# A hybrid encoder layer on one core: the next down weights' transfers go through ScalarE's queue a period later, the last two pairs' activation lows through VectorE, and the next group's sums behind them

## The chip, the cores and the metric

One core of one Trainium2 chip runs the whole layer. The metric is device time in microseconds (us) of one execution. The time before is the median of three runs, 820.84 us (819.92 to 821.39). The profile is of one further execution of the same program.

## What is computed

The reference is one encoder layer on 512 positions of width 1024, in float32:

```
x = x + 0.5 * (silu(h1 @ w_gate1) * (h1 @ w_up1)) @ w_down1      # h1 = RMSNorm(x), d_ff = 2752
h = RMSNorm(x); u = h @ w_in                                     # Fourier group, q, k, v
x = x + concat([fourier_mixer(u), gqa_attention(u)]) @ w_out
x = x + 0.5 * (silu(h2 @ w_gate2) * (h2 @ w_up2)) @ w_down2      # h2 = RMSNorm(x)
y = RMSNorm(x)
```

The change touches only the two feed-forward parts (FFN 1 and FFN 2).

## The kernel before

**High and low parts.** Every matrix product is made of float32r operands split in two: a high part (a rounded copy) and a low part (the value less its high part). A weight tile comes from HBM as a raw float32 tile. ScalarE casts it to the high part (line 182 for down weights, 404 for gate and up weights). The low part is made in one of two ways. `lows` (line 140) has VectorE subtract the high part from the raw value. `rest_by_dma` (lines 169 and 170) has ScalarE write the negated high part, and GpSimd issues a DMA that adds the raw value onto it on the way.

**Pairs and groups.** The 2752 hidden columns are 21 pairs of 128 gate and 128 up columns, and a tail. They are taken in four groups for each FFN (lines 38 and 39). The first group is multiplied plainly. In the other three, `seven` (line 440) multiplies each pair by a seven-product scheme on half-blocks: the products are P0 to P5 and P9, written to banks r, p, q and c (lines 449 and 452), and four sums of weight blocks (`c1` to `c4` of `prepare`, line 419) are their operands. P0 of a pair needs the block a11, of which the low part comes by the accumulating DMA (tile `ring<-raw_g`). One pair takes TensorE one period of somewhat over 9 us. The `TABLE` (line 46) lists the steps of one period; a `+` behind a name means the step of the next pair, a `-` the one of the pair before. ScalarE, VectorE and GpSimd keep this order; TensorE and SyncE keep the order in which the code is written; outside the table a scheduler places the instructions.

**Down products.** When a group's pairs are through, their activations (tile `at`, high and low part, from u by lines 518 and 521 or 522) are multiplied by the down weights of the group, eight blocks d = 0 to 7 (`dn` on line 196, 18 products for a block of six pairs), and added to x (line 629). The raw down weights, `raw_dn_d`, share three buffers (tag "raw", line 163) with the raw up weights, `raw_u`, in the order in which the code asks for them. The raw gate weights, `raw_g`, have two buffers of their own.

**Around the end of a group.** In `seven`, `i` counts the pairs of the group and `len(js)` is their number. At P0 of the last pair (line 531) `load_below` asks SyncE for raw_dn 0 and 1. At the table's `c3+` in the last period and at its `t.h` in the extra half period behind it (`BELOW`, lines 43 and 533), `below` makes the casts and lows of down blocks 0 and 1. The low part of an activation is the table's step `nh`: it comes by accumulating DMA (tile `at<-u`, line 522), except for the last pair of a group, and the last two of an FFN's last group, which take VectorE (line 543). The next group's first pair is prepared during the down products, its steps (`FIRST`, line 45) tied by `behind` (line 619) to come after the instructions in `anchors`: ScalarE's copy pA and VectorE's sum lB of the last pair.

Of the kernel before, what the change touches and what calls it, by code (L numbers as in the profile page):

```python
# [18 lines left out]
KD = D // P  # L19
# [20 lines left out]
PLACES = 7  # L40
HALF = S // 2
USES = "a11", "a12", "s2", "s1", "s4", "s3", "a22"
BELOW = "t.h", "c3"
HELD = 2
FIRST = ("ld", "a.h", "a.l", "c1", "d.h", "d.l", "c2", "c3", "c4", "s.h", "s.l", "t.h", "t.l")
TABLE = """
# [47 lines left out]
def asf(ap):  # L94
    return ap.bitcast(F32)
# [3 lines left out]
def encoder(ctx, tc, A, out):  # L99
    nc = tc.nc  # L100
# [38 lines left out]
    def lows(lo, src, hi):  # L139
        return nc.vector.tensor_tensor(out=lo, in0=src, in1=asf(hi), op=ALU.subtract)  # L140
# [17 lines left out]
    def weight_slots(n=KD, skip=0):  # L158
        c = slice(skip, skip + n * P)
        return (slot()[:, c].rearrange("p (a b) -> p a b", b=P) for _ in range(2))  # L160

    def raw_tile(src, name, n=KD):
        raw = wp.tile([P, KD, P], F32, tag="raw", name=f"raw_{name}")
        nc.sync.dma_start(out=raw[:, :n, :], in_=src)
        return raw

    def rest_by_dma(lo, hi, src):

        nc.scalar.activation(lo, asf(hi), AF.Copy, scale=-1.0)  # L169
        nc.gpsimd.dma_start(out=lo, in_=src, accum_op=ALU.add)  # L170
# [5 lines left out]
    def weights(src, name, n=KD, raw=None, by_dma=False, skip=0):  # L176
        raw = raw or raw_tile(src, name, n)
        hi, lo = weight_slots(n, skip)
        if name in HI_DVE:
            nc.vector.tensor_copy(hi[:, :n, :], raw[:, :n, :])  # L180
        else:
            nc.scalar.copy(hi[:, :n, :], raw[:, :n, :])  # L182
        if by_dma:
            rest_by_dma(lo, hi, src)
        else:
            lows(lo[:, :n, :], raw[:, :n, :], hi[:, :n, :])
        return hi, lo

    def turned(ap):
# [104 lines left out]
    def ffn(norm, after, wgu, wd, wdt, groups, opening, closing):  # L294
# [4 lines left out]
        n_ = norm.n  # L299
        n_plain = len(groups[0])  # L300
        with tc.tile_pool(name=f"act{n_}", bufs=1) as ap, tc.tile_pool(name=f"sums{n_}", bufs=2) as sp:
# [8 lines left out]
            def place(j):  # L310
                where[j] = free.pop(0)
                return where[j]
# [8 lines left out]
            def gate(c, between={}, by_dma=False):  # L321
                with ExitStack() as behind:
                    for i in (norm.squared, norm.added) if n_ and c else ():
                        behind.enter_context(tc.issue_after(i.ins))
                    whi, wlo = weights(wgu[c], f"gu{n_}_{c}", by_dma=by_dma)
                ps = bank(f"gu{n_}_{c}")
                for k in range(KD):
                    between.get(k, int)()
                    product(ps, whi[:, k, :], wlo[:, k, :], hh[k], hl[k], k == 0, k == KD - 1, turn=True)
                return ps  # L330
# [38 lines left out]
            def back(ts):  # L369
                plain[:] = [t for t in plain if all(t is not q for q in ts)]  # L370
# [67 lines left out]
            anchors = {}  # L438

            def seven(js, first, finish, load_below, below):  # L440
# [86 lines left out]
                def do(i, name):  # L527
                    shift = name.count("+") - name.count("-")
                    name = name.rstrip("+-")
                    i += shift  # L530
                    if i == len(js) - 1 and name == "P0":
                        load_below()
                    if i == len(js) and name in BELOW:
                        below()
                    if i not in range(len(js)):
                        return
                    o = state.setdefault(i, {})
                    if "w" not in o:
                        o.update(prepare(js[i]))
                    if "P0" not in o:  # L540
                        o.update(evacuation(js[i], o))
                    if i and (i, name) != (1, "ld") or not i and name not in FIRST:
                        o["l" if name == "nh" and i >= len(js) - 1 - last else name]()
                    if i == 0 and name == "P0":
                        finish()

# [6 lines left out]
                def rest():  # L553
                    for name in ended:
                        do(len(js), name)

                return rest

            def down_raw(d, group, gi):

                js = [j for j in group if j != "t"]
                return raw_tile(wd[d][:, js[0] : js[-1] + 1, :], f"dn{n_}_{d}_{gi}", len(js))

            def down(d, group, gi):

                js = [j for j in group if j != "t"]
                src, halves_ = wd[d][:, js[0] : js[-1] + 1, :], closing and gi == len(groups) - 1 and d >= KD - LAST
                raw = raws[d] = loads.pop(0) if loads else down_raw(d, group, gi)
                whi, wlo = weights(src, "", len(js), raw, skip=SKIP if halves_ else 0)
                if halves_:  # L570
                    token_weights(d, js)
                w = wt[d // 4][:, d % 4 * P : (d % 4 + 1) * P]

                def steps(ps, t):
                    for i, j in enumerate(group):
                        h, l = (at[:, where[j], o, t] for o in range(2))
                        first, last = i == 0, i == len(group) - 1
                        turn = t == every
                        if j == "t":
                            o, h, l = (turned(p) if turn else p for p in (ps[:, t], h, l))  # L580
                            nc.tensor.matmul(o, w, h, start=first, stop=False)
                            nc.tensor.matmul(o, w, l, start=False, stop=last)
                        else:
                            k = j - js[0]
                            cut = first and d == KD - LAST and t == slice(0, HALF)
                            product(ps[:, t], whi[:, k, :], wlo[:, k, :], h, l, first, last, cut, turn)
                        yield

                return steps
# [44 lines left out]
            for gi, group in enumerate(groups):  # L634
                last = gi == len(groups) - 1
                ahead = []
                if gi:
                    downs, loads = [], []
                    rest = seven(
                        range(group[0] + 1, min(group[-1] + 2, NF)), ready, finish,  # L640
                        lambda: loads.extend(down_raw(d, group, gi) for d in range(2)),
                        lambda: downs.append(down(len(downs), group, gi)),
                    )
                else:
                    downs, loads = [], []
                    lent = [acts[:, FRONT + i * KD * P : FRONT + (i + 1) * KD * P] for i in range(PLACES - 4, PLACES)]
                    plain.extend(lent)
                    row = []
                    pss = dict(enumerate(opening(gate, lambda: norm.column([norm.acc]), lambda: row.append(norm.row()))))
                    back(lent[:2])  # L650
                    due, parts, left = [*pss, "t"], list(range(KH)), range(2 * len(pss), 2 * n_plain)
                    pss["t"] = [gate(2 * NF)]
                    tail_weights()
                    for i, c in enumerate(left):
                        pss.setdefault(c // 2, []).append(gate(c, by_dma=i in (1,) if n_ else i > 0))
                        if due:
                            j = due.pop(0)
                            evacuate(at[:, place(j)], n_, pss[j], norm)
                        if c % 2 and c != left[-1]:
                            due.append(c // 2)  # L660
                        while len(parts) * len(left) > (len(left) - 1 - i) * KH:
                            o = parts.pop(0)
                            operands(row[0], o, o + 1)

                    def rest():
                        done = evacuate(at[:, place(n_plain - 1)], n_, pss[n_plain - 1], norm)
                        if n_:
                            anchors["DVE"] = done
# [9 lines left out]
                for d in range(KD):  # L678
# [26 lines left out]
                    def finish(waiting=waiting, added=added if last or d < KD - 1 else lambda d, ps: residual(d, ps, every)):  # L705
                        for d_, ps, steps in waiting:
                            for _ in steps:
                                pass
                            added(d_, ps)
# [130 lines left out]
    with in_order():  # L840
        ffn(n0, n1, A["wgu1"], A["wd1"], A["wdt1"], GROUPS1, opening1, None)
# [684 lines left out]
    with in_order():  # L1526
        ffn(n2, n3, A["wgu2"], A["wd2"], A["wdt2"], GROUPS2, lambda gate, column, row: [[gate(0, {KD - 1: column}), gate(1, {3: row})]], closing)
# [122 lines left out]
```

## Time and profile before

| | |
|---|---|
| median of three runs | 820.84 us (819.92 to 821.39) |
| the profiled execution | 820.24 us |
| its span, first to last instruction | 818.5 us |
| VectorE busy | 640.1 us (78%) |
| ScalarE busy | 548.8 us (67%) |
| GpSimd busy | 81.8 us (10%) |
| granted TensorE clock | 1.000 |

Times in the views are us from the span's start; PE is TensorE, DVE VectorE, ACT ScalarE, POOL GpSimd, SPq SyncE's queue. A row of the timeline has start, duration, engine, line, operation, tiles and, in brackets, the idle time before it and what ended it. Where a later instruction starts before the end of an earlier one of its engine, the two overlap in the pipeline. The view of DMA issues has the size of one transfer and the us from issue to landing.

### The profile page before, as it was taken

Reading aid. Unit: us, or ns where it says so; the run is one execution under the profiler, and the core shown is the slowest. Engines: PE = TensorE matmul, PEld = TensorE weight load, DVE = VectorE, ACT = ScalarE, POOL = GpSimd, SP = SyncE. Lnnn points to the kernel's source line nnn. Section 1 sums busy time; section 2 is a strip of 40 time slices with the busy share of each in tenths; the row PEclk is TensorE's granted clock in tenths of the full one; section 3 lists DMA queues with packets and bytes.
Section 4 is the critical chain, followed back from the end, with each engine's and each line's share of the span. In section 5 each row is a group of like instructions: output and inputs, shape, how many; then the busy total and the mean of one; then the engine's idle time right before and its main releaser. Section 6 shows DMA issues by size and latency. Waiting matters only on the chain.

```text
span 818.5 us, 11871 instructions
## 1 busy us (share of the span) xinstructions
PE 807.1 (99%) x4376; PEld 706.0 (86%) x4376; DVE 640.1 (78%) x1073; ACT 548.8 (67%) x874; POOL 81.8 (10%) x93
## 2 busy tenths in 40 slices
PE   9999999999999999999999999999999999999997
PEld 7888988888888888889988888889888988888886
DVE  7996988388865867799998588989783998389774
ACT  7774876278735845779999457578643876278562
POOL 0120210011100100111000001102100110011001
PEclk9999999999999999999999999999999999999999
DMA  7675885559554833352110316778563785459322
GB/s 258 175 166 161 188 201 136 158 136 212 117 193 90 180 90 116 104 168 77 60 53 26 103 53 160 153 196 203 130 180 103 178 200 137 156 128 218 72 94 103
DMA packets 40491, 115.29 MB, mean 141 GB/s; under 512 B 4720, under 2 KB 10224, under 8 KB 40432
## 3 DMA queue, kind: packets, MB, share of 16 engines
q1 hardware_dynamic: 27776, 82.61, 32.9%
q0 software_dynamic: 11936, 30.94, 20.4%
q10 hardware_dynamic: 720, 0.98, 0.3%
q8 instruction: 34, 0.56, 0.3%
q14 instruction: 25, 0.20, 0.1%
HBM read 84.24 MB, written 2.10 MB: 105 GB/s over the span
## 4 chain that ended last, share of the span: by engine, by line
PE 90%; DMA 8%; issue 0%; DVE 0%; ACT 0%; POOLq 0%; POOL 0%; DVEq 0%
PE dn L196 25%; PE r L449 12%; PE mix L196 9%; PE gu L196 8%; DMA ring<-raw_g 7%; PE r L452 7%; PE p L449 3%; PE c L449 3%; PE q L449 3%; PE gu L806 3%; PE mix L1306 2%; PE mix L1266 2%; PE p L452 2%; PE q L452 2%; PE c L452 2%; PE mix L1104 1%
## 5 line engine op out<-in xcount | busy, mean ns | idle before, releaser
L196 PE MATMUL dn<-at,ring 128*128 128x512 f32 x900 | 203.3, 380 | 0.0
L196 PEld LDWEIGHTS dn<-at,ring 128*128 128x128 f32 x900 | 167.6, 188 | 28.8
L449 PE MATMUL r<-rt,ring 128*128 128x512 f32 x560 | 191.5, 383 | 0.0
L452 PE MATMUL r<-rt,ring 128*128 128x256 f32 x560 | 153.7, 275 | 4.4 <-DMA ring<-raw_g 4.4
L449 PEld LDWEIGHTS r<-rt,ring 128*128 128x128 f32 x560 | 105.1, 188 | 18.8
L452 PEld LDWEIGHTS r<-rt,ring 128*128 128x128 f32 x560 | 105.2, 188 | 6.7 <-DMA ring<-raw_g 6.3
L629 DVE SCALAR_TENSOR_TENSOR gx<-dn,gx 128x512 f32<-128x512 f32 x61 | 41.7, 687 | 71.7 <-PE dn L196 71.6
L140 DVE TENSOR_TENSOR ring<-s,ring 128x1024 fp32r<-128x1024 f32 x70 | 85.3, 1219 | 2.5 <-ACT ring L404 0.6
L182 ACT CAST ring<-raw_dn 128x768 fp32r<-128x768 f32 (+3 forms) x58 | 44.9, 781 | 57.9 <-PE dn L196 49.1
L404 ACT CAST ring<-s 128x1024 fp32r<-128x1024 f32 x70 | 73.0, 1043 | 7.4 <-PE p L449 5.6
L140 DVE TENSOR_TENSOR ring<-raw_dn,ring 128x768 fp32r<-128x768 f32 (+3 forms) x58 | 51.6, 892 | 14.7 <-ACT ring L182 13.7
L170 POOL DMA_DIRECT2D ring<-raw_g x35 | 30.1, 859 | 247.3 <-ACT ring L169 177.5
L485 ACT COPY p<-r 128x512 f32<-128x512 f32 x35 | 19.9, 570 | 47.9 <-PE r L452 47.9
L169 ACT ACTIVATE ring<-ring 128x1024 fp32r<-128x1024 f32 x38 | 40.3, 1059 | 13.9 <-PE dn L196 12.5
L196 PE MATMUL gu<-ring 128*128 128x512 f32 x216 | 48.9, 381 | 0.0
L449 PE MATMUL p<-rt,ring 128*128 128x512 f32 x140 | 48.5, 383 | 0.0
L449 PE MATMUL q<-rt,ring 128*128 128x512 f32 x140 | 48.4, 382 | 0.0
L449 PE MATMUL c<-rt,ring 128*128 128x512 f32 x140 | 48.4, 382 | 0.0
L196 PEld LDWEIGHTS gu<-ring 128*128 128x128 f32 x216 | 40.4, 188 | 6.9
L404 ACT CAST ring<-raw_g 128x1024 fp32r<-128x1024 f32 x35 | 36.8, 1050 | 10.3 <-DMA raw_g<-in_wgu 10.3
L170 POOL DMA_DIRECT2D at<-u x27 | 23.2, 858 | 185.0 <-ACT p L505 185.0
L459 DVE TENSOR_TENSOR u<-u,r 128x256 f32<-128x256 f32 x70 | 29.4, 421 | 13.1 <-ACT u L512 11.9
(282 smaller groups left out, 1712.4 us busy)
## 6 DMA issues: line engine op xcount, KB each, us to landing
raw_g<-in_wgu SPq DMA_DIRECT2D x35, 512.0 KB, 4.0
raw_u<-in_wgu SPq DMA_DIRECT2D x35, 512.0 KB, 5.2
ring<-raw_g POOLq DMA_DIRECT2D x35, 512.0 KB, 7.6
raw_dn<-in_wd SPq DMA_DIRECT2D x40, 384.0 KB, 3.7
at<-u POOLq DMA_DIRECT2D x27, 256.0 KB, 3.9
raw_gu<-in_wgu SPq DMA_DIRECT2D x12, 512.0 KB, 3.8
raw_o<-in_wo SPq DMA_DIRECT2D x8, 512.0 KB, 3.3
raw_dn<-in_wd SPq DMA_DIRECT2D x8, 448.0 KB, 4.1
```

Of the source, the lines that this page charges most:

```text
L140: return nc.vector.tensor_tensor(out=lo, in0=src, in1=asf(hi), op=ALU.subtract)
L169: nc.scalar.activation(lo, asf(hi), AF.Copy, scale=-1.0)
L170: nc.gpsimd.dma_start(out=lo, in_=src, accum_op=ALU.add)
L182: nc.scalar.copy(hi[:, :n, :], raw[:, :n, :])
L196: nc.tensor.matmul(ps, a, b, start=first and b is mhi and a is whi, stop=last and a is wlo)
L404: nc.scalar.copy(hi, src())
L449: nc.tensor.matmul(turned(ps), whi[:, ks], turned(m), start=first and i == 0, stop=False, skip_group_check=True)
L452: nc.tensor.matmul(turned(ps[:, :HALF]), wlo[:, ks], turned(m[:, :HALF]), start=False, stop=i == KH - 1, skip_group_check=True,)
L459: return nc.vector.tensor_tensor(out=out, in0=a, in1=b, op=ALU.add)
L485: nc.scalar.copy(o[key], o["r"])
L629: nc.vector.scalar_tensor_tensor(out=x[d][:, t], in0=ps[:, t], scalar=0.5, in1=x[d][:, t], op0=ALU.mult, op1=ALU.add)
L806: nc.tensor.matmul(turned(pss[c]), w[:, k % 2, c], turned(m[k]), start=k == 0 and m is hh and w is hi, stop=k == KD - 1 and w is lo,)
```

## The change

Three edits, all at the end of groups two to four of each FFN.

1. Raw down weights 0, 1 and 2 are issued from ScalarE's queue and not from SyncE's, each at a place of its own in the table (`LOADS`): block 0 at `a.h+` of the last period, block 1 at `c2+` of it, block 2 at `s.h` of the half period behind it. Before, blocks 0 and 1 were asked for together, at P0 of the last period, and block 2 after the next group's first gate and up weights. Since ScalarE works its instructions off in order, the transfers now start when it gets there.
2. The activation low of the last two pairs is made by VectorE in every such group. That is one pair more in four groups.
3. Casts and lows of down block 1 stand at `t.l` of the half period (`t.h` in the kernel before), and the last cast and low of `below` become anchors: the sums and casts of the next group's first pair are scheduled behind them.

```diff
-BELOW = "t.h", "c3"
+LOADS = "a.h", "s.h", "c2"
+BELOW = "t.l", "c3"
...
+    cast = {}
+
+    def raw_tile(src, name, n=KD, by=nc.sync):
         raw = wp.tile([P, KD, P], F32, tag="raw", name=f"raw_{name}")
-        nc.sync.dma_start(out=raw[:, :n, :], in_=src)
+        by.dma_start(out=raw[:, :n, :], in_=src)
...
-            nc.scalar.copy(hi[:, :n, :], raw[:, :n, :])
+            cast["ACT"] = nc.scalar.copy(hi[:, :n, :], raw[:, :n, :])
...
-            lows(lo[:, :n, :], raw[:, :n, :], hi[:, :n, :])
+            cast["DVE"] = lows(lo[:, :n, :], raw[:, :n, :], hi[:, :n, :])
...
-                    if i == len(js) - 1 and name == "P0":
+                    if i == len(js) and name in LOADS:
                         load_below()
                     if i == len(js) and name in BELOW:
                         below()
+                        anchors.update(cast)
...
-                        o["l" if name == "nh" and i >= len(js) - 1 - last else name]()
+                        o["l" if name == "nh" and i >= len(js) - 2 else name]()
...
-            def down_raw(d, group, gi):
+            def down_raw(d, group, gi, by=nc.sync):
...
-                        lambda: loads.extend(down_raw(d, group, gi) for d in range(2)),
+                        lambda: loads.append(down_raw(len(loads) + len(downs), group, gi, nc.scalar)),
```

TensorE's instructions keep their order. The other queues change as follows, shown for the second group of FFN 1 (pairs 4 to 9). In the rows, `raw_dn_0_1` is down block 0 of that group, `raw_g_10` and `raw_u_10` are the next group's first weights, and the last number of a name is a counter. Lines of the changed kernel stand three or four higher.

SyncE's queue before, from the raw up weights of the last pair on:

```order
L393 DMA raw_u_9_1048<-in_wgu 128x1024
L164 DMA raw_dn_0_1_1185<-in_wd 128x768
L164 DMA raw_dn_1_1_1187<-in_wd 128x768
L393 DMA raw_g_10_1332<-in_wgu 128x1024
L393 DMA raw_u_10_1333<-in_wgu 128x1024
L164 DMA raw_dn_2_1_1337<-in_wd 128x768
L164 DMA raw_dn_3_1_1362<-in_wd 128x768
```

and in the changed kernel:

```order
L396 DMA raw_u_9_1048<-in_wgu 128x1024
L396 DMA raw_g_10_1333<-in_wgu 128x1024
L396 DMA raw_u_10_1334<-in_wgu 128x1024
L167 DMA raw_dn_3_1_1361<-in_wd 128x768
L167 DMA raw_dn_4_1_1387<-in_wd 128x768
```

Three down loads left this queue. In the order of the three "raw" buffers raw_u_10 now follows raw_dn_2 instead of raw_dn_1, so it takes over the buffer of raw_dn_0 instead of raw_u_9.

ScalarE's queue before, from the cast of the activation of the last pair but one (pair 8):

```order
L518 CAST at_128<-u_8_1181 128x512
L169 ACTIVATE at_128<-at_128 128x512
L505 COPY p_9_1257<-q_9_1238 128x256
L182 CAST ring<-raw_dn_0_1_1185 128x768
L404 CAST ring<-raw_g_10_1332 128x1024
L404 CAST ring<-raw_u_10_1333 128x512
L169 ACTIVATE ring<-ring 128x1024
L509 ACTIVATE g_9_1231<-g_9_1231 128x512
L182 CAST ring<-raw_dn_1_1_1187 128x768
L182 CAST ring<-raw_dn_2_1_1337 128x768
L404 CAST ring<-s_0_10_1411 128x1024
```

and in the changed kernel:

```order
L521 CAST at_128<-u_8_1181 128x512
L508 COPY p_9_1254<-q_9_1236 128x256
L167 DMA raw_dn_1_1_1256<-in_wd 128x768
L185 CAST ring<-raw_dn_0_1_1194 128x768
L167 DMA raw_dn_2_1_1274<-in_wd 128x768
L512 ACTIVATE g_9_1229<-g_9_1229 128x512
L185 CAST ring<-raw_dn_1_1_1256 128x768
L407 CAST ring<-raw_g_10_1333 128x1024
L407 CAST ring<-raw_u_10_1334 128x512
L185 CAST ring<-raw_dn_2_1_1274 128x768
L172 ACTIVATE ring<-ring 128x1024
L515 COPY u_9_1270<-r_9_1185 128x256
```

The negated copy of pair 8 is gone, two DMA issues came in around the cast of down block 0 (that of block 0 stands a period earlier, behind the copy p of pair 8), and the next group's casts stand behind the cast of block 1.

VectorE's queue before, from the low of down block 0:

```order
L140 TENSOR_TENSOR ring<-raw_dn_0_1_1185,ring 128x768
L459 TENSOR_TENSOR p_9_1257<-p_9_1257,q_9_1238 128x256
L459 TENSOR_TENSOR g_9_1231<-c_9_1233,p_9_1257 128x256
L459 TENSOR_TENSOR u_9_1271<-r_9_1189,p_9_1257 128x256
L459 TENSOR_TENSOR u_9_1271<-u_9_1271,r_9_1189 128x256
L459 TENSOR_TENSOR g_9_1231<-g_9_1231,c_9_1233 128x256
L419 TENSOR_TENSOR s_0_10_1411<-raw_u_10_1333 128x512
L140 TENSOR_TENSOR ring<-raw_u_10_1333,ring 128x512
L419 TENSOR_TENSOR s_0_10_1481<-raw_g_10_1332,raw_u_10_1333 128x512
L419 TENSOR_TENSOR s_0_10_1411<-s_0_10_1411,raw_g_10_1332 128x512
L140 TENSOR_TENSOR ring<-raw_dn_1_1_1187,ring 128x768
```

and in the changed kernel, the last rows of the same stretch and what follows them:

```order
L462 TENSOR_TENSOR g_9_1229<-g_9_1229,c_9_1231 128x256
L141 TENSOR_TENSOR ring<-raw_dn_1_1_1256,ring 128x768
L422 TENSOR_TENSOR s_0_10_1410<-raw_u_10_1334 128x512
L422 TENSOR_TENSOR s_0_10_1480<-raw_g_10_1333,raw_u_10_1334 128x512
L633 SCALAR_TENSOR_TENSOR gx<-dn_0_1_1280,gx 128x512
L141 TENSOR_TENSOR ring<-raw_u_10_1334,ring 128x512
L422 TENSOR_TENSOR s_0_10_1410<-s_0_10_1410,raw_g_10_1333 128x512
L141 TENSOR_TENSOR ring<-raw_dn_2_1_1274,ring 128x768
```

The low of down block 1 now stands ahead of everything that reads raw_u_10, and five instructions that need raw_u_10 or stand among those that do are between it and the low of block 2. The added low of pair 8's activation stands one row ahead of the low of block 0.

More of the change, by code (lines that the diff above doesn't have):

```diff
@@ L160, in weight_slots @@
         return (slot()[:, c].rearrange("p (a b) -> p a b", b=P) for _ in range(2))
-    def raw_tile(src, name, n=KD):
+    cast = {}
+    def raw_tile(src, name, n=KD, by=nc.sync):
         raw = wp.tile([P, KD, P], F32, tag="raw", name=f"raw_{name}")
-        nc.sync.dma_start(out=raw[:, :n, :], in_=src)
+        by.dma_start(out=raw[:, :n, :], in_=src)
         return raw
@@ L557, in seven @@
                 return rest
-            def down_raw(d, group, gi):
+            def down_raw(d, group, gi, by=nc.sync):
                 js = [j for j in group if j != "t"]
-                return raw_tile(wd[d][:, js[0] : js[-1] + 1, :], f"dn{n_}_{d}_{gi}", len(js))
+                return raw_tile(wd[d][:, js[0] : js[-1] + 1, :], f"dn{n_}_{d}_{gi}", len(js), by)
             def down(d, group, gi):
```

## The prediction

> **What bounds the kernel now.** I read the page first, then the waits of TensorE, then the timeline and the DMA issues around one such wait. The page:
>
> ```profile
> span 818.5 us, 11871 instructions
> PE 807.1 (99%) x4376; PEld 706.0 (86%) x4376; DVE 640.1 (78%) x1073; ACT 548.8 (67%) x874; POOL 81.8 (10%) x93
> ```
>
> TensorE is busy for 99% of the span, and the change leaves its instructions and their order alone. So it can only win what TensorE waits. In the view of waits (total, times, longest) the first row stands for nearly all of that (the second is the start):
>
> ```profile
> PE r L452 <- DMA ring<-raw_g: 4.4, 6, 1.2
> PE busy L751 <- PEq L1633: 0.8, 1, 0.8
> ```
>
> Six waits, one for each group worked by seven products, all for the accumulating DMA that makes the low part of a11. The timeline of TensorE at the first:
>
> ```profile
> 109.50 0.38 PE L449 MATMUL r<-rt,ring 128*128 128x512 f32 x1
> 109.72 0.28 PE L452 MATMUL r<-rt,ring 128*128 128x256 f32 x1
> 109.83 0.39 PE L449 MATMUL r<-rt,ring 128*128 128x512 f32 x1
> 110.73 0.38 PE L452 MATMUL r<-rt,ring 128*128 128x256 f32 x1 [0.51 <-DMA ring<-raw_g]
> 110.95 0.39 PE L449 MATMUL r<-rt,ring 128*128 128x512 f32 x1
> ```
>
> The undisturbed step from one L449 to the next is 109.83 - 109.50 = 0.33 us; across the wait it is 110.95 - 109.83 = 1.12 us. The wait costs 0.79 us, 0.28 more than the idle time in brackets, because the modelled ends of matmuls hide the rest. If the other five hide as much (an estimate from this one), the six cost 4.4 + 6 x 0.28 = 6.1 us. This is P0 of pair 8, the last but one of its group, and the low part was wanted at 109.83 + 0.22 = 110.05.
>
> Why is it late there and nowhere else? The DMA issues of that period; then the a11 DMA of one period earlier (at 91.7 us, with raw_g and raw_u beside it and no raw_dn) and of one later (at 110.4); then the worst of the six (at 189.6 us, third group); then the slowest that met no down load (at 635.6 us). The last column is us to landing:
>
> ```profile
> raw_g<-in_wgu SPq DMA_DIRECT2D x1, 512.0 KB, 3.9
> raw_u<-in_wgu SPq DMA_DIRECT2D x1, 512.0 KB, 5.6
> ring<-raw_g POOLq DMA_DIRECT2D x1, 512.0 KB, 9.6
> raw_dn<-in_wd SPq DMA_DIRECT2D x1, 384.0 KB, 9.0
> ...
> ring<-raw_g POOLq DMA_DIRECT2D x1, 512.0 KB, 8.1
> ...
> ring<-raw_g POOLq DMA_DIRECT2D x1, 512.0 KB, 7.6
> ...
> ring<-raw_g POOLq DMA_DIRECT2D x1, 512.0 KB, 10.3
> raw_dn<-in_wd SPq DMA_DIRECT2D x1, 384.0 KB, 10.0
> ...
> ring<-raw_g POOLq DMA_DIRECT2D x1, 512.0 KB, 9.0
> ```
>
> With gate and up weights beside it the a11 DMA takes 8.1 us; with 384 KB of down weights besides, 9.6. SyncE asks for down block 0 as soon as a raw buffer comes free, two periods ahead of its use, and so right into the a11 transfer. GpSimd's rows tell when each a11 DMA is issued, SyncE's when the next group's up weights are:
>
> ```profile
> 101.06 0.86 POOL L170 DMA_DIRECT2D ring<-raw_g  x1 [1.45 <-ACT ring L169]
> 110.40 0.86 POOL L170 DMA_DIRECT2D ring<-raw_g  x1 [1.45 <-ACT ring L169]
> 130.98 0.86 POOL L170 DMA_DIRECT2D ring<-raw_g  x1 [2.56 <-ACT ring L169]
> ...
> 118.62 0.33 SPq L393 DMA_DIRECT2D raw_u<-in_wgu  x1
> ```
>
> The late one left at 101.06 and was wanted at 110.05, so it may take 8.9 us.
>
> **The change, part by part.** *Down block 0 out of the a11 transfer.* Its DMA now stands on ScalarE behind the copy p of pair 8, the row at 117.84 below. The a11 DMA issued at 101.06 then has only the companions of the period before: 8.1 us instead of 9.6, under the 8.9 that are allowed. Taken off the worst, the same 1.5 us give 8.8. So all six waits go, -6.1 us. The bound on the other side: if each still took the 9.0 us of the undisturbed row, 0.1 us of idle and 0.28 behind it would stay, 6 x 0.38 = 2.3 us, and the gain is 3.8. I take 6.1, since the direct neighbour has 8.1. What would be late next must come from the group's end, below: PE's other waits are the start's.
>
> *Three DMA issues on ScalarE, one negated copy less.* ScalarE's rows at the end of the group, then the same place in the fourth group (where the negated copy was already absent), then what two issues on ScalarE's queue cost at the start:
>
> ```profile
> 117.84 0.36 ACT L505 COPY p<-q 128x256 f32<-128x256 f32 x1
> 121.50 0.57 ACT L485 COPY p<-r 128x512 f32<-128x512 f32 x1 [2.35 <-PE r L452]
> 125.98 0.62 ACT L518 CAST at<-u 128x512 fp32r<-128x512 f32 x1
> 127.17 0.35 ACT L505 COPY p<-q 128x256 f32<-128x256 f32 x1
> 127.43 0.83 ACT L182 CAST ring<-raw_dn 128x768 fp32r<-128x768 f32 x1
> 131.80 0.82 ACT L182 CAST ring<-raw_dn 128x768 fp32r<-128x768 f32 x1
> ...
> 294.68 0.62 ACT L518 CAST at<-u 128x512 fp32r<-128x512 f32 x1
> 295.53 0.37 ACT L505 COPY p<-q 128x256 f32<-128x256 f32 x1 [0.23 <-PE q L452]
> ...
> 0.74 0.89 ACTq L745 DMA_DIRECT2D raw_first<-in_first  x2
> ```
>
> The first issue lies in the 2.35 us idle before 121.50. The second stands before the cast of block 0. It costs 0.89 / 2 = 0.45 us (at most 0.86, by GpSimd's rows); without the negated copy the copy p comes 0.85 us behind the cast of at (295.53 - 294.68) instead of 1.19, which saves 0.34. The cast of block 0 moves by +0.1 us (at most +0.5). Who waits for it:
>
> ```profile
> 128.29 0.96 DVE L140 TENSOR_TENSOR ring<-raw_dn,ring 128x768 fp32r<-128x768 f32 x1 [2.44 <-ACT ring L182]
> 131.15 0.68 DVE L419 TENSOR_TENSOR s<-raw_u 128x512 f32<-128x512 f32 x1
> ...
> 132.95 0.69 DVE L419 TENSOR_TENSOR s<-s,raw_g 128x512 f32<-128x512 f32 x1
> 133.56 0.95 DVE L140 TENSOR_TENSOR ring<-raw_dn,ring 128x768 fp32r<-128x768 f32 x1
> ...
> 129.30 4.14 PE L196 MATMUL dn<-at,ring 128*128 128x512 f32 x18
> 134.64 4.56 PE L196 MATMUL dn<-at,ring 128*128 128x512 f32 x20
> ```
>
> VectorE ends the low of block 0 at 129.25; TensorE wants it for the third product, at 129.30 + 2 x 0.22 = 129.74. The slack of 0.49 holds +0.1, and at +0.5 it just goes: cost 0, at most 6 x 0.1 us.
>
> *One activation low more on VectorE, in four groups.* About 0.69 us (the row at 132.95 is of that size) in the 2.44 us that VectorE idles before 128.29: cost 0. If that cover were gone, 4 x 0.69 = 2.8 us would bound it. The accumulating DMA that it replaces goes away too.
>
> *Down blocks 1 and 2 later.* Block 1 leaves at about 127.2 and its cast stands at 131.80, so 4.6 us are left for it. With the next group's casts and sums queued behind it (edit 3), its low can follow its cast at about 132.7 to 133.6, ahead of the 134.64 + 0.44 = 135.08 where TensorE wants it. Two rows for such loads, a down block and a raw_u almost alone, and the slowest raw_u of all:
>
> ```profile
> raw_dn<-in_wd SPq DMA_DIRECT2D x1, 384.0 KB, 3.2
> ...
> raw_u<-in_wgu SPq DMA_DIRECT2D x1, 512.0 KB, 3.8
> ...
> raw_u<-in_wgu SPq DMA_DIRECT2D x1, 512.0 KB, 8.3
> ```
>
> Block 1 in 3.2 us is in time; late it would be from 6.1 us on (135.08 less 0.95 and 0.83 for low and cast, less 127.2).
>
> *The next group's up weights.* They had raw_u_9's buffer and left SyncE at 118.62. Now they have down block 0's, so they leave when VectorE ends its low, at 129.3. The sums that read them block VectorE's queue: behind them wait x's sum of block 0, and the low of block 2. From their landing VectorE needs five instructions at 0.60 us (131.15 to 133.56 are four in 2.41) and 0.96, together 4.0 us, and TensorE wants that low at 134.64 + 18 x 0.22 + 0.44 = 139.0 (one product starts each (4.14 - 0.38) / 17 = 0.22 us). So they must land by 135.0, 5.7 us after issue. Alone a raw_u took 3.8 us; beside down blocks 1 and 2, issued about 2 and 1 us ahead of it, I add up to the 1.5 us that 384 KB cost above: 3.8 to 5.3. In time: cost 0.
>
> The Trainium skill (DMA: Bandwidth & Descriptors, Rules for kernel authors) speaks against these two parts: issue a DMA early and wait for it late, so that its fixed cost is covered. The rows at 101.06 and above show the reverse side here, an early load that delays another. By the rule alone the sum would be a loss, worked out as the second rival below.
>
> *Sum.* 820.24 - 6.1 = 814.1 us for the profiled execution. The median of the runs is 0.6 above it (820.84), so 814.7 us.
>
> **The rivals.** *Part of the waits stays.* If the backlog of gate, up and a11 transfers makes 9.0 us as in the last row of that fence, the gain is 3.8 and the time 820.84 - 3.8 = 817.0. For it: that row; against it: the neighbours of the first wait have 8.1 and 7.6. Chance 0.09.
>
> *The next up weights come late (slower).* Their lead shrinks from over 12 us (118.62 to 131.15) to about 4.3 (129.3 to 133.6), and what waits is the low of block 2, at the four group ends that a further group follows. It decides from 5.7 us to landing on; at 5.7 + 6.1 / 4 = 7.2 us the gain is used up; at the slowest row, 8.3 us, it is 4 x (8.3 - 5.7) = 10.4 us, and 820.84 - 6.1 + 10.4 = 825.1 us. Against it: that slowest row had an a11 DMA beside it, and the next one now leaves after 130.98. Chance 0.07, of which 0.02 for an end within 0.2%.
>
> *Only the queue changes.* If the a11 DMA was slowed by something else than the down load, or the load still met one, nothing is won: 820.8 us. The Trainium skill (DMA: Bandwidth & Descriptors, Issuing engines are not separate DMA queues) says that transfers from any queue share the same 16 DMA engines and interleave, so that a change of queue alone gives no bandwidth. The trace agrees: the a11 DMA and the down load of the first fence, on two queues, land together. But no a11 DMA is in flight from 110.40 + 7.6 = 118.0 to 130.98, and the first down load cannot leave before 117.84, so it is the later time that helps. Chance 0.04.
>
> **How the numbers follow.** The forecast, 814.7 us, has the remaining 0.80. The runs before lie up to 0.9 us below their median, and the 0.28 is known from one wait: low end 813.4. The high end takes in the first rival and the same spread upwards, 817.0 + 1.0 = 818.0. What a measurement of this kernel can tell from no change is 0.2%, 1.6 us. Faster by more: 0.80 + 0.09 = 0.89. Within it: 0.04 + 0.02 = 0.06. Slower: 0.05.
>
> **What would show it.** In the profile of the changed kernel the row `PE r L452 <- DMA ring<-raw_g` should be gone, the six a11 DMAs should land in 7.5 to 8.8 us, TensorE should be busy all but the span's ends, and the span should be near 812.4. A wait of PE `dn` for VectorE's or ScalarE's `ring` at the start of down blocks 1 or 2, with VectorE idle for raw_u before, would show the second rival. If the a11 DMAs land as late as before although no raw_dn is issued beside them, the step from the down load to the late landing is wrong.

## The result, and the profile after

The changed kernel takes 815.75 us (median of six runs, 815.35 to 816.77), beside 820.31 us for six runs of the kernel before on the same chip. The ratio is 0.9944, with a 95% interval of 0.9932 to 0.9957: 4.6 us faster. The forecast was 814.7 us, a gain of 6.1; by the interval the gain is 3.5 to 5.6. On a second chip the changed kernel had 815.8 us against 819.88, a ratio of 0.9955 (0.9942 to 0.9969).

The page and TensorE's waits of the changed kernel (total, times, longest). The profiled execution is the slowest of the six, 816.77 us:

```profile
span 815.0 us, 11838 instructions
PE 807.5 (99%) x4376; PEld 706.7 (87%) x4376; DVE 643.0 (79%) x1077; ACT 546.5 (67%) x870; POOL 78.4 (10%) x89
...
PE r L455 <- DMA ring<-raw_g: 0.6, 2, 0.4
```

The busy time of TensorE is the same as before; what it waits for the a11 DMA went from 4.4 us in six places to 0.6 in two. In the second profiled execution (of the other chip, 815.70 us) it is gone: the first row of its waits is the start's.

```profile
span 813.9 us, 11838 instructions
...
PE busy L755 <- PEq L1637: 0.8, 1, 0.8
```

The first down load now leaves ScalarE's queue at 117.29 us. The a11 DMA that was late before leaves at 101.65 and has landed 8.1 us later, at 109.7:

```profile
101.65 0.86 POOL L173 DMA_DIRECT2D ring<-raw_g  x1 [1.45 <-ACT ring L172]
...
117.29 0.34 ACTq L167 DMA_DIRECT2D raw_dn<-in_wd  x1
```

TensorE at the place of the first wait, in the first of these two executions. The step from one L452 to the next is 110.42 - 110.08 = 0.34 us; nothing is left of the 1.12 us step before.

```profile
110.08 0.38 PE L452 MATMUL r<-rt,ring 128*128 128x512 f32 x1
...
110.42 0.38 PE L452 MATMUL r<-rt,ring 128*128 128x512 f32 x1
```

The largest wait that stayed is in the third group of FFN 1. Its a11 DMA and its companions of that period (KB, us to landing), and TensorE:

```profile
raw_g<-in_wgu SPq DMA_DIRECT2D x1, 512.0 KB, 3.8
ring<-raw_g POOLq DMA_DIRECT2D x1, 512.0 KB, 9.8
raw_u<-in_wgu SPq DMA_DIRECT2D x1, 512.0 KB, 8.0
...
198.54 0.39 PE L452 MATMUL r<-rt,ring 128*128 128x512 f32 x1
199.29 0.38 PE L455 MATMUL r<-rt,ring 128*128 128x256 f32 x1 [0.36 <-DMA ring<-raw_g]
```

No raw_dn is among them, and the DMA still took 9.8 us (10.3 before). In the other execution the same DMA took 9.2 us and TensorE did not wait (its run below tells why). What made it 9.8 is open.

The six a11 DMAs in question, us from issue to landing, in the order of the groups (from the DMA issues of each execution; the last five rows are experiments told below):

| kernel | FFN 1 | FFN 2 | mean |
|---|---|---|---|
| before | 9.6, 10.3, 9.9 | 10.2, 9.8, 9.3 | 9.9 |
| changed | 8.1, 9.8, 8.6 | 9.4, 8.3, 7.9 | 8.7 |
| changed, other chip | 8.0, 9.2, 9.0 | 9.3, 8.3, 7.9 | 8.6 |
| load of block 0 early again | 9.4, 10.7, 10.6 | 10.3, 9.4, 9.5 | 10.0 |
| late places, from SyncE | 9.4, 10.2, 9.9 | 10.0, 9.5, 9.4 | 9.7 |
| without the first edit | 9.3, 10.0, 9.6 | 9.6, 9.3, 9.3 | 9.5 |
| the first edit alone | 8.0, 8.9, 8.8 | 9.4, 8.0, 8.4 | 8.6 |
| five activation lows by VectorE | 7.4, 8.7, 6.8 | 8.6, 7.6, 7.8 | 7.8 |

The four kernels with an early down load have means of 9.5 to 10.0, the others of the table of 7.8 to 8.7.

Where the time went, product by product: both executions have the same 4376 products in the same order, so the difference of their starts shows each place at which time is won or lost. From before to the first execution of the changed kernel the six waits shrank by 4.9 us in all; the start came 0.6 us later, 0.4 us is a new small wait for the a11 DMA one pair ahead of the 199 us one (9.2 us, 7.5 before), and 0.4 us was lost in steps that were slower without a wait. That is -3.5, the difference of the spans. To the other chip's execution the waits shrank by 5.6, the start gained 0.2 and slower steps took 1.2: -4.6.

The group's end went as worked out. VectorE in the changed kernel, with the up weights' issue on SyncE and TensorE's two down blocks:

```profile
126.42 0.69 DVE L141 TENSOR_TENSOR at<-u,at 128x512 fp32r<-128x512 f32 x1 [0.78 <-ACT at L521]
127.92 0.96 DVE L141 TENSOR_TENSOR ring<-raw_dn,ring 128x768 fp32r<-128x768 f32 x1 [0.81 <-ACT ring L185]
...
132.27 0.96 DVE L141 TENSOR_TENSOR ring<-raw_dn,ring 128x768 fp32r<-128x768 f32 x1 [1.42 <-ACT ring L185]
133.15 0.69 DVE L422 TENSOR_TENSOR s<-raw_u 128x512 f32<-128x512 f32 x1
...
128.91 0.33 SPq L396 DMA_DIRECT2D raw_u<-in_wgu  x1
...
129.09 4.15 PE L199 MATMUL dn<-at,ring 128*128 128x512 f32 x18
134.42 4.78 PE L199 MATMUL dn<-at,ring 128*128 128x512 f32 x21
```

The added low (126.42) fits into VectorE's idle time, the low of block 0 ends at 128.88, ahead of TensorE's 129.09, and the low of block 1 at 133.23, 1.2 us ahead of 134.42. The up weights left at 128.91 and landed 4.1 us later, at 133.04: VectorE takes them at 133.15, straight behind the low of block 1.

### The profile page after: what moved, and what is told of

It is laid out like the page before. It is cut to its first block, busy times and chain, and to the rows that moved or that the text cites. A ratio compares the mean times of both kernels' runs of the same rounds, so it can differ in the third digit from the quotient of the medians.

```text
span 815.0 us, 11838 instructions
## 1 busy us (share of the span) xinstructions
PE 807.5 (99%) x4376; PEld 706.7 (87%) x4376; DVE 643.0 (79%) x1077; ACT 546.5 (67%) x870; POOL 78.4 (10%) x89
## 4 chain that ended last, share of the span: by engine, by line
PE 94%; DMA 4%; issue 0%; ACT 0%; DVE 0%; POOLq 0%; POOL 0%; DVEq 0%
PE dn L199 26%; PE r L452 14%; PE mix L199 9%; PE gu L199 8%; PE r L455 7%; PE p L452 3%; DMA ring<-raw_g 3%; PE q L452 3%; PE c L452 3%; PE gu L810 3%; PE p L455 2%; PE mix L1310 2%; PE q L455 2%; PE c L455 2%; PE mix L1270 2%; PE mix L1108 1%
## 5 line engine op out<-in xcount | busy, mean ns | idle before, releaser
L452 PE MATMUL r<-rt,ring 128*128 128x512 f32 x560 | 191.5, 383 | 0.0
L452 PEld LDWEIGHTS r<-rt,ring 128*128 128x128 f32 x560 | 105.1, 188 | 19.0
L452 PE MATMUL p<-rt,ring 128*128 128x512 f32 x140 | 48.6, 383 | 0.0
L452 PE MATMUL q<-rt,ring 128*128 128x512 f32 x140 | 48.5, 383 | 0.0
L452 PE MATMUL c<-rt,ring 128*128 128x512 f32 x140 | 48.5, 383 | 0.0
L455 PE MATMUL p<-rt,ring 128*128 128x256 f32 x140 | 38.3, 274 | 0.0
L455 PE MATMUL q<-rt,ring 128*128 128x256 f32 x140 | 38.3, 273 | 0.0
```

Of the source, the lines that this page charges most:

```text
L452: nc.tensor.matmul(turned(ps), whi[:, ks], turned(m), start=first and i == 0, stop=False, skip_group_check=True)
L455: nc.tensor.matmul(turned(ps[:, :HALF]), wlo[:, ks], turned(m[:, :HALF]), start=False, stop=i == KH - 1, skip_group_check=True,)
```

## The experiments

All but the first are edits of the changed kernel. Each was timed beside runs of the kernel before on its own chip; times are medians, ratios go against the kernel before.

### The changed kernel again

> The changed kernel once more, beside the next three. By the first comparison 0.9944 of the time before, about 815.8 us; its profile shows whether the two or three small waits for the a11 DMA that were left (third group of the first layer, second of the second) are those places again, or fall anywhere.

815.8 us, 0.9955 (0.9942 to 0.9969). The waits that were left are a matter of margin: the slowest a11 DMAs fall in the same two groups (9.2 and 9.3 us), but here no wait for them is listed. That is in part luck. The one of 9.2 us left at 188.58, and TensorE reached the product that needs it at 197.84:

```profile
188.58 0.86 POOL L173 DMA_DIRECT2D ring<-raw_g  x1 [1.44 <-ACT ring L172]
...
197.84 0.38 PE L455 MATMUL r<-rt,ring 128*128 128x256 f32 x1
```

Those are 9.26 us, where the first group before had 110.05 - 101.06 = 8.99. TensorE's steps in between were slower in this execution (the last section tells of such stretches), and the same holds in the other group. At the usual pace both DMAs would have come 0.2 to 0.3 us late.

### The load of block 0 early again, from ScalarE

The only instruction that moves in each group is one DMA on ScalarE's queue. The rest of the edit asks for the weights of the last pair ahead of it, so that SyncE's loads keep their order.

```diff
-LOADS = "a.h", "s.h", "c2"
+LOADS = "s.h", "c2"
...
+                    if (i, name) == (len(js) - 3, "f1"):
+                        do(i + 2, "ld")
+                        load_below()
...
```

> The changed kernel, with one DMA moved: down block 0's load still leaves from ScalarE's queue, but two periods earlier, behind the cast of the sums of the pair before (about 102.2 us in the first such group, where the kernel before had it at 101.6 on SyncE). Main theory (the time of this load, beside the a11 DMA, makes the waits): the six a11 DMAs take 9.3 to 10.3 us again, TensorE waits about 4 us for them, and the time is 815.75 + 4.6 = 820.3 us (819.3 to 821). Rival A (the queue: SyncE's own transfers held the a11 DMA up, ScalarE's would not): 815.8 us. Rival B (the gain came from the added low on VectorE and the new order behind it, not from the load): 815.8 us.

822.08 us, 1.0025 (1.0013 to 1.0037): 6.3 us more than the changed kernel, slower than before, and 1.1 us over the main theory's range. TensorE's waits, and the DMAs of that period in the first such group:

```profile
PE r L455 <- DMA ring<-raw_g: 5.3, 6, 1.6
...
raw_g<-in_wgu SPq DMA_DIRECT2D x1, 512.0 KB, 4.7
raw_u<-in_wgu SPq DMA_DIRECT2D x1, 512.0 KB, 7.7
ring<-raw_g POOLq DMA_DIRECT2D x1, 512.0 KB, 9.4
raw_dn<-in_wd ACTq DMA_DIRECT2D x1, 384.0 KB, 5.3
```

All six waits are back. One load of 384 KB, at an early time, makes them, from whichever queue. The DMA left at 100.33 us, 0.5 us ahead of the a11 DMA (before: 0.5 behind it), and the others took longer beside it: raw_g 4.7 instead of 3.9 us in the changed kernel, raw_u 7.7 instead of 5.7. That earlier start may be why the waits are longer than the theory had them (5.3 us and not 4); it was not tested apart. Both rivals, the queue and the other two edits, gave 815.8 and fall.

### The loads at the late places, from SyncE

```diff
-lambda: loads.append(down_raw(len(loads) + len(downs), group, gi, nc.scalar)),
+lambda: loads.append(down_raw(len(loads) + len(downs), group, gi)),
```

> The changed kernel, with the three loads of down blocks 0 to 2 at the same places of the program but on SyncE's queue. Main theory: SyncE has nothing else to wait for, so it asks for block 0 as soon as a raw buffer is free, about 101.5 us, beside the a11 DMA; the waits are back, 820.3 us, or more (up to 825) since the next group's gate weights now stand behind block 2 on SyncE and leave some 8 us later. Rival (the place in the program is enough, whatever the queue): 815.8 us.

819.42 us, 0.9994 (0.9984 to 1.0004). TensorE's waits, and SyncE's queue around the first:

```profile
PE r L455 <- DMA ring<-raw_g: 3.3, 5, 1.1
...
100.85 0.46 SPq L396 DMA_DIRECT2D raw_u<-in_wgu  x1
101.42 17.11 SPq L167 DMA_DIRECT2D raw_dn<-in_wd  x3
```

The first of the three loads leaves at 101.42, beside the a11 DMA, as before: on SyncE, which has no other work, the new places in the code do not make it later. The time is 0.9 us under the 820.3 that the main theory gave as the least, and the next group's gate weights, which now leave only at 118.62, show in no wait of TensorE. So ScalarE's queue matters only for the time at which the load is asked for. An engine that is busy with its own work in order asks for the load when it gets there; SyncE asks as soon as a buffer is free.

### Without the first edit

The casts and lows of block 1 go back to `t.h` too; the added low and the anchors stay.

```diff
-LOADS = "a.h", "s.h", "c2"
-BELOW = "t.l", "c3"
+BELOW = "t.h", "c3"
...
-                    if i == len(js) and name in LOADS:
+                    if i == len(js) - 1 and name == "P0":
...
-lambda: loads.append(down_raw(len(loads) + len(downs), group, gi, nc.scalar)),
+lambda: loads.extend(down_raw(d, group, gi) for d in range(2)),
```

> The changed kernel without its first part: down blocks 0 to 2 are loaded from SyncE as in the kernel before; the added low on VectorE and the new order behind the cast and low of block 1 stay. Main theory (the gain is the load's): six waits of TensorE for the a11 DMA, 4.4 us idle in all, 820.3 us. Rival (the other two parts carry some of the gain): between 815.8 and 820.3, with those waits shorter.

819.6 us, 0.9998 (0.9987 to 1.0009). Six waits are there, five at the places of before and one a pair earlier (second group of FFN 2):

```profile
PE r L454 <- DMA ring<-raw_g: 2.1, 6, 0.8
```

The added low and the anchors gain nothing by themselves that these runs can tell. The 2.1 us are less than the 4.4 of before, but this profile is of the fastest of its runs (817.28 us, 2.3 below the median), so it doesn't show that they shorten the waits.

### Without the second edit

```diff
-o["l" if name == "nh" and i >= len(js) - 2 else name]()
+o["l" if name == "nh" and i >= len(js) - 1 - last else name]()
```

> The changed kernel without its second part: in four groups the last pair but one's activation low comes again from a negated copy on ScalarE and an accumulating DMA. That DMA would leave at about 127.6 us in the first such group, beside the loads of down blocks 1 and 2 (126.6 and 127.1), and TensorE wants the low at 129.09 + 15 x 0.22 = 132.4, so it may take 4.8 us. Theory 1 (it is slowed by the two loads: 3.3 us alone, 1.5 more for each 384 KB): up to 6.3 us, up to 1.5 us of wait at four group ends, 817 to 821.8 us, with waits of TensorE's dn for the DMA of at. Theory 2 (the prediction's: this part costs and brings nothing by itself): 815.8 us.

819.12 us, 1.0002 (0.9985 to 1.0018): the gain is lost. TensorE's waits, the worst place, and the DMAs issued there from 676 to 679 us:

```profile
PE dn L199 <- DMA at<-u: 1.9, 2, 1.7
...
684.40 0.71 PE L199 MATMUL dn<-at,ring 128*128 128x512 f32 x2 [1.68 <-DMA at<-u]
...
raw_dn<-in_wd ACTq DMA_DIRECT2D x2, 384.0 KB, 3.5
raw_u<-in_wgu SPq DMA_DIRECT2D x1, 512.0 KB, 5.6
at<-u POOLq DMA_DIRECT2D x1, 256.0 KB, 7.1
```

This profile is of the fastest of the twelve runs (817.75 us). Here the activation's 256 KB took 7.1 us beside the late loads and the up weights; left at 677.25, they were wanted at 682.54, so 5.3 were allowed, and the same transfer took 4.7 us in the kernel before. At the four group ends in order the transfer took 3.3, 3.3, 3.6 and 4.7 us before and takes 5.1, 5.5, 5.1 and 7.1 here. By the starts of the products TensorE loses 0, 0.4, 0.6 and 2.0 us there. Theory 1 holds: the late loads move the crowd to the group's end, and the DMA that stood there has to go.

### Without the third edit

Only its anchors go; block 1 stays at `t.l`, and what that place does alone was not tried.

```diff
-                        anchors.update(cast)
```

> The changed kernel without its third part: the next group's casts and sums aren't queued behind down block 1's cast and low, so on VectorE three sums that read raw_u stand ahead of the low of block 1. Main theory: raw_u lands at 133.0 in the first such group, three sums of 0.6 us end at 134.9, the low of block 1 at 135.8, and TensorE wants it at 134.42 + 0.44 = 134.86: about 0.95 to 1.2 us of wait at each of four group ends, 819.5 to 820.6 us. Rival (that part is idle, TensorE has room there): 815.8 us.

819.52 us, 0.9994 (0.9984 to 1.0003). TensorE's waits; VectorE and TensorE at the end of the third group:

```profile
PE dn L199 <- DVE ring L141: 2.2, 3, 0.9
...
221.25 0.69 DVE L422 TENSOR_TENSOR s<-raw_u 128x512 f32<-128x512 f32 x1 [2.20 <-DMA raw_u<-in_wgu]
...
222.46 0.68 DVE L422 TENSOR_TENSOR s<-s,raw_g 128x512 f32<-128x512 f32 x1
223.06 0.95 DVE L141 TENSOR_TENSOR ring<-raw_dn,ring 128x768 fp32r<-128x768 f32 x1
...
224.07 2.27 PE L199 MATMUL dn<-at,ring 128*128 128x512 f32 x9 [0.85 <-DVE ring L141]
```

VectorE stands idle for 2.20 us until the up weights land, makes the next group's three sums, and only then the low of block 1, for which TensorE waits. This is the second rival's mechanism, one block earlier than it was told; the anchors of the third edit keep it away.

### The first edit alone

The edits of the last two experiments together; `t.l` stays here too.

> The first part of the change alone: down blocks 0 to 2 from ScalarE's queue at the later places; the activation's negated copy and DMA stay, and nothing is queued behind the cast and low of block 1. Theory 1 (the losses without the third part, 819.5 - 815.8 = 3.7 us, and without the second, 819.1 - 815.8 = 3.3 us, are of different waits and add up): 815.8 + 3.7 + 3.3 = 822.8 us, slower than before, with TensorE's dn waiting for VectorE's ring and for the DMA of at. Theory 2 (they overlap, since a TensorE that waits for the one finds the other done): 819.5 to 820.5 us. The prediction, which gave the second and the third part no worth of their own: 815.8 us.

824.39 us, 1.0065 (1.005 to 1.008): slower than before. TensorE's waits:

```profile
PE dn L199 <- DVE ring L141: 3.2, 3, 1.6
PE dn L199 <- DMA at<-u: 1.9, 2, 1.3
...
PE r L455 <- DMA ring<-raw_g: 0.2, 1, 0.2
```

The a11 waits are gone but for 0.2 us, and both new ones are there. They add up, and a bit more (8.6 us above the changed kernel, where the two single ones were 3.8 and 3.3).

### Three more activation lows on VectorE

```diff
-o["l" if name == "nh" and i >= len(js) - 2 else name]()
+o["l" if name == "nh" and i >= len(js) - 5 else name]()
```

> The changed kernel with three more activation lows a group on VectorE instead of a negated copy and an accumulating DMA (the last five pairs instead of the last two). The changed kernel still waits 0.6 us idle in three places for the a11 DMA, which lands in 9.2 to 9.8 us there. Theory 1 (256 KB of an activation's DMA beside it are part of that: 384 KB cost 1.5 us, so 256 KB about 1.0): those a11 DMAs come under 8.9 us, the waits go, 815.75 - 0.6 - 3 x 0.28 = 814.3 us. Theory 2 (the gate and up weights alone make it so long): 815.8 us. Theory 3 (18 more lows at 0.69 us on VectorE delay the sums that the products need): slower, 817 to 820 us, with waits of TensorE for VectorE's ring.

819.97 us, 0.9996 (0.9987 to 1.0006), and yet no a11 wait is left in TensorE's waits. The a11 DMAs came down to 7.8 us in the mean, as theory 1 had it. But theory 3 outweighs it. TensorE and VectorE in one of the pairs whose low was moved, and the group of those products (busy us, mean ns | idle us before them):

```profile
101.35 0.27 PE L455 MATMUL r<-rt,ring 128*128 128x256 f32 x1
101.67 0.49 PE L452 MATMUL r<-rt,ring 128*128 128x512 f32 x1
102.00 0.27 PE L455 MATMUL r<-rt,ring 128*128 128x256 f32 x1
...
97.47 0.69 DVE L141 TENSOR_TENSOR at<-u,at 128x512 fp32r<-128x512 f32 x1
...
101.19 0.42 DVE L462 TENSOR_TENSOR u<-u,r 128x256 f32<-128x256 f32 x1
...
L452 PE MATMUL r<-rt,ring 128*128 128x512 f32 x560 | 193.9, 386 | 0.7
```

The product at 101.67 starts a new sum in bank r, which VectorE's sum reads until 101.61. It starts 0.32 us behind the product before it, and the next one 0.33 behind that, where such steps are 0.11 and 0.22 (see the rows at 109.50 to 109.83 in the prediction): 0.31 us for each of 18 pairs, 5.6 us in all, by the starts of the products. The median rose by 4.2 us: the a11 waits that were left are gone besides, and the rest of the difference is open. The matmuls' modelled ends hide this from the waits: the last row has only 0.7 us of idle time for all 560 products.

### The a11 DMA ahead of the activation's

```diff
-P0 a.h+ a.l+ s.h f1 si- s.l P9- vA- c1+ vB- P1
+P0 a.h+ a.l+ nk-- s.h f1 si- s.l P9- vA- c1+ vB- P1
...
+                    if name in ("nh", "nk"):
+                        if (i < len(js) - 2) != (name == "nk"):
+                            return
+                        name = "nh"
```

> The changed kernel with the negated copy of an activation (0.63 us on ScalarE) moved behind the one of a11, so that each a11 DMA leaves about 0.6 us earlier and the activation's DMA behind it instead of ahead. Theory 1 (the waits that are left are a margin of under 1 us: 9.2 to 9.8 us against 8.9 allowed): they go, about 814.3 us. Theory 2 (the activation's 256 KB, now wholly beside the a11 DMA where 60% of its time lay ahead of it, slow it by what the earlier start brought): 815.8 us, with a11 DMAs of 0.5 to 1 us longer.

819.88 us, 1.0000 (0.9992 to 1.0009). Neither theory gives this time: the a11 waits are gone, as theory 1 has it, but another takes their place. TensorE's waits, and VectorE:

```profile
PE r L452 <- DVE u L462: 1.9, 3, 0.9
...
200.72 0.42 DVE L462 TENSOR_TENSOR u<-r,p 128x256 f32<-128x256 f32 x1 [1.59 <-DMA at<-u]
```

The activation's DMA adds tile u, which has two buffers, onto the low. It lands later now, so the buffer comes free later, and VectorE's next sum into it, which reads bank r out for TensorE's next use, waits 1.59 us. Compared start by start with the changed kernel on the same chip, TensorE loses 4.9 us at eleven such places; most of that is hidden from the list. Whether a third buffer of u would take the wait away, and the order then win, was not tried.

## Why the prediction was right, and where its size was off

**The cause.** The down load beside the a11 DMA was the step on which all rested. It stands shown: one such DMA moved back brings all six waits (the early load from ScalarE), and taking it away from there removes them, whatever else goes wrong (the first edit alone: 0.2 us left). The forecast that the queue as such does nothing is shown by the same pair of kernels. The Trainium skill (DMA: Bandwidth & Descriptors, Issuing engines are not separate DMA queues) says the same, that DMAs of any queue interleave on the same engines; the 9.4 us beside a load from ScalarE, against 9.6 beside one from SyncE, agree.

**The size, 4.6 us and not 6.1.** Three terms of the sum were off. First, 8.1 us was taken from the neighbours of the first wait for all six; the six measured 7.9 to 9.8 (mean 8.7), and in two groups 9.2 to 9.8 is over the 8.99 that are allowed. That is the first rival's mechanism, in two groups of six. It was worth 0.7 us in one execution, and 0.4 more one pair ahead; in the other slower steps of TensorE hid it. Second, the 0.28 us behind each idle time, known from one wait, was too much: where no wait was left, the six steps shrank by 5.6 and not 6.1. Third, slower steps took 0.4 to 1.2 us back, which the sum did not hold at all; nothing ties them to the change. These three are read from two executions, of 816.77 and 815.70 us. The time was missed by 1.05 us, less than the gain, and that is luck: the sum started from a median of 820.84 us of three runs, which is 820.31 for six.

**The group's end.** The issues on ScalarE cost nothing (the cast of block 0 began at 127.06, 2.03 us ahead of TensorE's down block at 129.09; before, at 127.43, 1.87 ahead), the up weights landed after 4.1 us (3.8 to 5.3 expected), and no wait of `dn` came up. Two costs at nothing were right as sums, but the working missed what they buy. The prediction weighed the added low on VectorE by its 0.69 us alone, and did not ask what the DMA that it replaces would do beside the late loads: 5.1 to 7.1 us, 3.3 us of the time. And it gave edit 3 only as the order in which block 1's low comes; without its anchors the time is 3.8 us longer.

**Early or late.** The Trainium skill (DMA: Bandwidth & Descriptors, Rules for kernel authors) has a DMA issued early and waited for late. Here the earlier issue of one load costs 6.3 us (822.08 against 815.75), because it displaces a transfer with less slack.

## What to carry to other kernels

A load with two periods of slack can still cost time: when a wait ends on a DMA, look at what else is in flight and which of it could go later, and queue that behind the work of an engine that gets there at the right time, not on a queue that runs ahead. Moving a transfer moves the crowd: list what is in flight at its new place and which instructions stand behind its consumer's queue, since here two of three edits do nothing but pay for the first. A list of waits can hide a loss that recurs; compare the starts of the same products in both executions.

## What the runs showed of the hardware

Steps of TensorE are not equally long where the views show no wait and the granted clock reads 1.00. In the other chip's execution of the changed kernel, one step at 109 us and one at 576 us, and the windows around them (us, busy times of the engines, clock, DMA share, GB/s):

```profile
109.25 0.38 PE L452 MATMUL r<-rt,ring 128*128 128x512 f32 x1
...
109.58 0.38 PE L452 MATMUL r<-rt,ring 128*128 128x512 f32 x1
...
575.96 0.39 PE L452 MATMUL r<-rt,ring 128*128 128x512 f32 x1
...
576.31 0.40 PE L452 MATMUL r<-rt,ring 128*128 128x512 f32 x1
...
100.00:110.00 10.00, 10.00 (x62) 9.00 (x61) 9.37 (x17) 8.93 (x15) 1.71 (x2) 1.00 0.89 197
571.00:581.00 10.00, 10.00 (x57) 8.46 (x57) 8.84 (x16) 7.57 (x13) 1.71 (x2) 1.00 0.70 161
```

The step is 0.33 us in the one and 0.35 in the other, for some 20 us. Such stretches cost about 0.5 us in the profiled execution of before (573 to 594 us) and 1.2 us more in this one. The first execution of the changed kernel and that of the late loads from SyncE lost the same 0.5 us at that place, the other seven nothing there; some of these lost as much elsewhere, the early load again at 280 to 300 us. The share of the DMA engines is lower at 576 us (0.70) than at 109 us (0.89). What makes the stretches is open.

The accumulating DMA was slowed most in company. Of the four transfers at 676 us without the second edit, the two down loads took 3.5 us (3.2 almost alone, in the prediction's row), the up weights 5.6 instead of the 4.6 that they took at that place of the changed kernel, and the accumulating one 7.1 instead of the 4.7 of the kernel before.

Some kernels in which TensorE waits for DMAs also vary more. Of those with eleven runs, the one without the first edit spread over 4.5 us, the one with the late loads from SyncE over 3.1 and the one without the anchors over 3.3; the two that have no a11 wait in the list, with five lows and with the a11 DMA first, over 1.7 and 1.5.
